# One joint block inverse for two recurrences, its diagonal blocks picked by DMA, and small work moved to GpSimd

## The chip, the cores and the metric

The kernel runs on one core of a Trainium2 chip. The metric is the device time of one execution in microseconds. Its engines are TensorE (PE; PEld is its weight load), VectorE (DVE), ScalarE (ACT), GpSimd (POOL) and SyncE (SP), which here issues all DMAs. Each runs its own queue of instructions in order, and waits at an instruction whose operands are not there.

## The reference

One step of a decoder layer for 1024 prompt tokens and 8 x 4 sample tokens. A projection `z = rmsnorm(x) @ w_in` feeds three mixers, whose outputs are gated, merged and followed by a feed-forward part. The change is in two of the mixers:

```
branch A (gated DeltaNet, 4 heads of 128 x 128, chunks of tokens)
  L    = strict_lower((k*beta) k^T * decay)      A = I + L
  u, w = A^-1 [v*beta | k*beta*exp(gc)]          attn = q k^T * decay
  per chunk:  vnew = u - w S;   o = (q exp(gc)) S + attn vnew
              S = S*exp(gc_last) + (k exp(gc_last - gc))^T vnew
branch B (RWKV-7, 8 heads of 64 x 64), per token
  S = S diag(w) - (S kk)(kk*a)^T + v k^T;   o = S r
  then group norm of o, bonus, gate
```

Branch B is solved by chunks of 64 tokens too, so each branch needs the inverse of unit triangular systems: 128 x 128 for each head and 128 tokens of A, 64 x 64 for each head and 64 tokens of B.

## The kernel before

Tokens lie along the free dimension, channels along partitions. `k.gemm` streams a weight in 128-column chunks through `wraw`; ScalarE and GpSimd split it in a high and a low half (`whi`, and `wlo` at L303), and TensorE takes three matmuls of 352 columns for each piece (L312 to L314, into PSUM tile `g`). These are the large products. Their chunks for the input projection and, later, for the merge gates are fed between the recurrences.

The recurrences run over two halves of the heads, and in each over nine segments: eight of 128 prompt tokens and one with the 32 sample tokens. `gdn_seg` is branch A's unit, two heads at once; `rwkv_seg` is branch B's, four blocks of two heads. That makes 18 pairs of units. Each unit has three parts, split by `yield`: the preparation with the block inverse `inv16`; the solve on top of it and the step of the state; and the output norm. The driver emits a unit's first part, then what is left of the unit before it, first for B and then for A. A scheduler then orders each engine's instructions from this order, so that instructions of different units and of the large products interleave.

`inv16` inverts the 16 x 16 diagonal blocks of all systems of a unit. VectorE masks the matrix to its diagonal blocks (L779), sums them to 16 columns (L782) and adds the unit diagonal (L783). A DMA writes the result to DRAM (L786) and another reads it back with each block's 256 numbers in all 16 partitions of the block (L788). Then 15 steps of a product (L795, tile `i16t`) and a sum (L796, tile `i16u`) give the inverse, row by row. `tri32` combines 16-blocks to 32-blocks by TensorE, and the code behind it goes on to 64 for B and to 128 for A. `inv16`, `tri32` and the tiles exist once with the suffix `r` (branch B) and once with `g` (branch A).

`rsqrt` is a Newton root, one instruction and three rounds of three (L592 to L594). It is used three times in a pair: for the keys' norms of A (tiles `nwyg`, `nwtg`), for A's output norm (`nwyo`, `nwto`) and for B's group norm (`nwyr`, `nwtr`). `BK` holds branch B's scaled keys. `LA` holds for each head of A the matrix L and the matrix attn side by side, `kv` its keys and values with tokens on partitions.

Of the kernel before, what the change touches and what calls it, by code (L numbers as in the profile page):

```python
# [95 lines left out]
def _consts():  # L96
# [33 lines left out]
    add("amk", np.where(p[:, None] > p[None], 0, NEG))  # L130
# [3 lines left out]
    add("amks", np.where(same4 & (t32[:, None] > t32[None]), 0, NEG))  # L134
# [238 lines left out]
def build(tc, ap):  # L373
    nc = tc.nc
    with ExitStack() as ctx:
# [209 lines left out]
        def rsqrt(x, shape, tag):  # L585

            yi = k.tile(mp, shape, "nwy" + tag, 2, I32)
            t = k.tile(mp, shape, "nwt" + tag, 1)
            V.tensor_scalar(out=yi, in0=x.bitcast(I32), scalar1=-0.5, scalar2=1597463007.0, op0=ALU.mult, op1=ALU.add)
            y = yi.bitcast(F32)  # L590
            for _ in range(3):
                V.tensor_tensor(out=t, in0=y, in1=y, op=ALU.mult)  # L592
                V.scalar_tensor_tensor(out=t, in0=t, scalar=-0.5, in1=x, op0=ALU.mult, op1=ALU.mult)
                V.scalar_tensor_tensor(out=y, in0=t, scalar=1.5, in1=y, op0=ALU.add, op1=ALU.mult)  # L594
            return y
# [63 lines left out]
        sc = c2.tile([128, 7, 9, 4], F32, name="sc")  # L659
        tg = c2.tile([128, 9, 4], F32, name="tg")  # L660
        for r, bs in ((128, slice(0, 8)), (32, slice(8, 9))):
            gc_, lb_ = gcb[:r, bs, :, 0], gcb[:r, bs, :, 1]
            A.activation(out=sc[:r, 0, bs], in_=gc_, func=AF.Exp, bias=k.c("lnh", r))
            A.activation(out=sc[:r, 1, bs], in_=lb_, func=AF.Exp, bias=k.c("lnh", r))
            V.scalar_tensor_tensor(out=sc[:r, 2, bs], in0=sc[:r, 0, bs], scalar=-2.0, in1=sc[:r, 1, bs], op0=ALU.mult, op1=ALU.mult)
            V.tensor_tensor(out=tg[:r, bs], in0=gla[:r, bs], in1=gc_, op=ALU.subtract)
            A.activation(out=sc[:r, 3, bs], in_=tg[:r, bs], func=AF.Exp, bias=k.c("lnh", r))
            V.tensor_copy(sc[:r, 4, bs], gc_)
            V.tensor_scalar(out=sc[:r, 5, bs], in0=gc_, scalar1=-1.0, scalar2=-2.0 * LN2, op0=ALU.mult, op1=ALU.add)
            V.tensor_scalar(out=sc[:r, 6, bs], in0=sc[:r, 1, bs], scalar1=0.5, scalar2=None, op0=ALU.mult)  # L670
# [98 lines left out]
        def inv16(fam, src, mask, nb, r, rows):  # L769


            srcs = src if isinstance(src, list) else [src]
            nq = srcs[0].shape[2]
            m = (k1() if fam == "r" else k.tile(mp, [128, SEG], "vv", 1))[:r, :nb * nq * 16]
            m = m.rearrange("p (b q c) -> p b q c", b=nb, q=nq)
            w = r // len(srcs)
            for i, a in enumerate(srcs):
                x = slice(w * i, w * i + w)
                V.tensor_tensor(out=m[x], in0=a, in1=mask[x].unsqueeze(1).unsqueeze(3).to_broadcast([w, nb, nq, 16]), op=ALU.mult)  # L779
            e16 = k.c("e16", r).unsqueeze(1).to_broadcast([r, nb, 16])  # L780
            c16 = k.tile(mp, [128, 4, 16], "i16c" + fam, 1)[:r, :nb]
            V.tensor_reduce(out=c16, in_=m.rearrange("p b q c -> p b c q"), axis=AXX, op=ALU.add)  # L782
            V.tensor_tensor(out=c16, in0=c16, in1=e16, op=ALU.add)  # L783
            k.n += 1
            dr = tc.dram_tile([r, nb * 16], F32, name=f"scr_i{k.n}")
            S.dma_start(dr, c16.rearrange("p b c -> p (b c)"))  # L786
            mb = k.tile(mp, [128, 1024 if fam == "r" else 512], "i16b" + fam, 1)[:r, :256 * nb]
# [18 lines left out]
        def tri32(fam, nb, l_of, transposed, u16):  # L806
# [735 lines left out]
```

## Time and profile before

| | us |
|---|---|
| median of 3 runs (lowest, highest) | 2314.09 (2312.11, 2326.05) |
| the profiled execution | 2314.56 |
| its span | 2312.8 |
| TensorE, VectorE, ScalarE, GpSimd busy in the span | 2203.3, 1310.6, 833.8, 303.7 |
| mean granted TensorE clock | 0.955 |

The span is the stretch from the first to the last instruction of the profiled execution. Busy time of an engine is the union of its instructions' durations. The two levels of TensorE's clock are 2.4 and 1.2 GHz, and a granted clock of 0.9 is a mean over both.

### The profile page before, as it was taken

How to read it: one execution, taken by the hardware profiler on the slowest of the kernel's cores; microseconds unless marked ns; L12 is line 12 of the kernel's file. 1: busy time of each engine (PE TensorE's matmuls, PEld its weight loads, DVE VectorE, ACT ScalarE, POOL GpSimd, SP SyncE). 2: the span in 40 equal slices, each digit the busy share in tenths (PEclk: the TensorE clock that was granted, in tenths of full speed). 3: DMA queues.
4: the chain of work that ended last, by engine and by line, in shares of the span. 5: the costliest groups of instructions: out<-in, count | busy, mean ns of one | idle time of the engine just before them, and what ended most of it. 6: DMA issues, size and time to landing. Idle time of an engine off the chain costs nothing. (4 is left out here: it accounts for less than half of the span.)

```text
span 2312.8 us, 43191 instructions
## 1 busy us (share of the span) xinstructions
PE 2203.3 (95%) x16747; PEld 2040.8 (88%) x16747; DVE 1310.6 (57%) x4204; ACT 833.8 (36%) x1969; POOL 303.7 (13%) x439
## 2 busy tenths in 40 slices
PE   8998998999998989899999999999999999999997
PEld 7998997777777767777799999989999999999997
DVE  7454247779888877787930167374333333343446
ACT  5466344344444434443432222253222122122234
POOL 3113222111121020111112100130000000000003
PEclk9999999789989988898999999999999999999999
DMA  4213224222323233223242354331111111111114
GB/s 144 67 60 101 100 99 119 87 87 79 98 79 99 81 107 91 84 73 85 77 142 93 124 196 140 122 113 44 46 48 47 46 47 46 46 46 46 46 49 150
DMA packets 138328, 199.82 MB, mean 86 GB/s; under 512 B 23880, under 2 KB 76488, under 8 KB 138124
## 3 DMA queue, kind: packets, MB, share of 16 engines
q1 hardware_dynamic: 138124, 197.07, 27.3%
q8 instruction: 132, 2.16, 0.4%
q14 instruction: 72, 0.59, 0.1%
HBM read 152.32 MB, written 44.70 MB: 85 GB/s over the span
## 5 line engine op out<-in xcount | busy, mean ns | idle before, releaser
L312 PE MATMUL g<-hhi,whi 128*128 128x352 f32 x2568 | 859.0, 335 | 11.2 <-DVE z L366 10.5
L314 PE MATMUL g<-hhi,wlo 128*128 128x352 f32 x2568 | 855.1, 333 | 0.9 <-POOL wlo L303 0.9
L313 PE MATMUL g<-hlo,whi 128*128 128x352 f32 x2472 | 822.6, 333 | 4.3 <-DVE hlo L505 2.6
L312 PEld LDWEIGHTS g<-hhi,whi 128*128 128x128 f32 x2568 | 493.0, 192 | 24.2 <-DVE z L366 12.5
L314 PEld LDWEIGHTS g<-hhi,wlo 128*128 128x128 f32 x2568 | 492.2, 192 | 10.8 <-issue 2.2
L313 PEld LDWEIGHTS g<-hlo,whi 128*128 128x128 f32 x2472 | 474.4, 192 | 15.0 <-DVE hlo L505 4.6
L302 ACT CAST whi<-wraw 128x512 fp32r<-128x512 f32 x326 | 201.3, 619 | 508.4 <-PE g L313 496.7
L303 DVE TENSOR_TENSOR wlo<-wraw,whi 128x512 fp32r<-128x512 f32 x216 | 151.6, 702 | 199.0 <-ACT whi L302 194.2
L312 PE MATMUL g<-ahi,whi 128*128 128x352 f32 x768 | 248.5, 324 | 0.0
L314 PE MATMUL g<-ahi,wlo 128*128 128x352 f32 x768 | 248.4, 323 | 0.0
L313 PE MATMUL g<-alo,whi 128*128 128x352 f32 x768 | 247.8, 323 | 0.0
L303 POOL TENSOR_TENSOR wlo<-wraw,whi 128x512 fp32r<-128x512 f32 x110 | 148.8, 1354 | 547.4 <-ACT whi L302 468.2
L1504 DVE TENSOR_TENSOR x<-g,x 128x352 f32<-128x352 f32 x192 | 100.3, 524 | 200.4 <-PE g L314 200.2
L1443 POOL TENSOR_TENSOR acc<-acc,sq 128x352 f32<-128x352 f32 x36 | 37.0, 1027 | 910.1 <-ACT sq L1442 743.8
L312 PEld LDWEIGHTS g<-ahi,whi 128*128 128x128 f32 x768 | 144.3, 188 | 0.2
L314 PEld LDWEIGHTS g<-ahi,wlo 128*128 128x128 f32 x768 | 144.3, 188 | 0.1
L313 PEld LDWEIGHTS g<-alo,whi 128*128 128x128 f32 x768 | 144.3, 188 | 0.1
L1493 DVE TENSOR_TENSOR rl<-rl,g 128x352 f32<-128x352 f32 x96 | 49.8, 518 | 130.9 <-ACT rl L1492 130.9
L1492 ACT ACTIVATE rl<-g 128x352 f32<-128x352 f32 x96 | 44.4, 463 | 136.3 <-PE g L314 136.3
L795 DVE TENSOR_TENSOR i16tr<-i16ur,i16br 128x8 f32<-128x8 f32 (+5 forms) x270 | 64.2, 238 | 38.0 <-DMA i16br<-scr_i 37.3
L1495 DVE TENSOR_TENSOR alo<-rl,ahi 128x352 fp32r<-128x352 f32 x96 | 50.3, 524 | 47.5 <-ACT ahi L1494 47.5
L1494 ACT CAST ahi<-rl 128x352 fp32r<-128x352 f32 x96 | 46.7, 487 | 63.2 <-DVE rl L1493 63.2
(383 smaller groups left out, 3048.8 us busy)
## 6 DMA issues: line engine op xcount, KB each, us to landing
wraw<-win SPq DMA_DIRECT2D x126, 256.0 KB
wraw<-wdn SPq DMA_DIRECT2D x80, 256.0 KB
wraw<-wup SPq DMA_DIRECT2D x64, 256.0 KB
scr_t<-z SPq DMA_DIRECT2D x24, 528.0 KB
tgl<-scr_t SPq DMA_DIRECT2D x24, 528.0 KB
scr_za<-z SPq DMA_DIRECT2D x16, 528.0 KB
i16br<-scr_i SPq DMA_DIRECT2D x16, 512.0 KB
wraw<-wout SPq DMA_DIRECT2D x32, 256.0 KB
```

The source lines that it names most:

```text
L302: self.A.copy(hi, r3)
L303: self.lo_eng.tensor_tensor(out=lo, in0=r3, in1=hi.bitcast(F32), op=ALU.subtract)
L312: T.matmul(ps, whi(k), xhi(k), start=start and k == ks[0], stop=False)
L313: T.matmul(ps, whi(k), xlo(k), start=False, stop=False)
L314: T.matmul(ps, wlo(k), xhi(k), start=False, stop=stop and k == ks[-1])
L795: V.tensor_tensor(out=t[:, :, 0:c + 1], in0=u[:, :, 0:c + 1], in1=w, op=ALU.mult)
L1443: (V if last else P).tensor_tensor(out=acc[g], in0=acc[g], in1=sq, op=ALU.add)
L1492: A.activation(out=rl, in_=ps, func=AF.Relu)
L1493: V.tensor_tensor(out=rl, in0=rl, in1=ps, op=ALU.mult)
L1494: A.copy(a[:, gl(g)], rl)
L1495: V.tensor_tensor(out=b[:, gl(g)], in0=rl, in1=a[:, gl(g)].bitcast(F32), op=ALU.subtract)
L1504: V.tensor_tensor(out=x2[c][:, gl(g)], in0=ps, in1=x2[c][:, gl(g)], op=ALU.add)
```

## The change

Branch A's system is now kept in transposed form, as B's has always been, so that one routine can treat the blocks of both. `gdn_seg` writes `LA` with one instruction for each head (matrix and attn share one exponential, whose sign is folded into the scalars), and leaves the key norm's scaling of `kv` to GpSimd. `inv16` and `tri` are called once for a pair. `inv16` no longer masks and sums: 16 DMAs copy the 16 x 16 diagonal blocks from `GM` and `LA` to DRAM, eight of each, and one DMA reads them back. The 15 steps run on six blocks at once, four of B and two of A (four in all in the two sample segments of B). `tri` does the two levels of the solve for all six, and the last level for A's 128 x 128 alone; its copies out of PSUM are shared between VectorE and ScalarE. The roots of A's output norm and of B's group norm, one of the two halves of `BK`, and the expansion of `X64` go to GpSimd, where each round of a root is four instructions. The driver emits B's preparation, then solve and state step of the older pair's B, then A's preparation, the joint inverse, and the older pair's A.

```diff
-        def rsqrt(x, shape, tag):
+        def rsqrt(x, shape, tag, E):
...
             for _ in range(3):
-                V.tensor_tensor(out=t, in0=y, in1=y, op=ALU.mult)
...
+                E.tensor_tensor(out=t, in0=y, in1=y, op=ALU.mult)
+                if E is V:
...
+                else:
+                    E.tensor_tensor(out=t, in0=t, in1=x, op=ALU.mult)
+                    E.tensor_scalar(out=t, in0=t, scalar1=-0.5, scalar2=1.5, op0=ALU.mult, op1=ALU.add)
+                    E.tensor_tensor(out=y, in0=t, in1=y, op=ALU.mult)
...
+        def inv16(J):
+            GM, LA, nb, nt = J["GM"], J["LA"], J["nb"], J["nb"] + 2
             k.n += 1
+            dr = tc.dram_tile([128, nt, 16], F32, name=f"scr_i{k.n}")
+            for g in range(8):
+                x = slice(16 * g, 16 * g + 16)
+                q = 16 * (g % 4)
+                S.dma_start(dr[x, 0:nb], GM[x, g // 4, 0:nb, q:q + 16])
+                S.dma_start(dr[x, nb:nt], LA[x, :, 0, 16 * g:16 * g + 16])
+            mb = k.tile(mp, [128, 1536], "i16b", 1)[:, :256 * nt]
+            S.dma_start(mb, dr.rearrange("(g k) b c -> g (k b c)", k=16).unsqueeze(1).to_broadcast([8, 16, 256 * nt]))
...
             for c in range(1, 16):
...
+                V.tensor_tensor(out=t[:, :, 0:c], in0=u[:, :, 0:c], in1=mb[:, 0:c, :, c].rearrange("p k b -> p b k"), op=ALU.mult)
                 V.tensor_reduce(out=u[:, :, c], in_=t[:, :, 0:c + 1], axis=AXX, op=ALU.add)
+            J["u16"] = u
...
+        def tri(J):
...
+            XT, X, y, z = tl("ixt"), tl("ix"), tl("iy"), tl("iz")
+            expand(XT, u16, k.c("h2"), nt, 2)
             V.transpose(out=w(X), in_=w(XT))
+            ps = rps32()
+            for b in range(nt):
                 for i in range(4):
+                    T.matmul(ps[Q[i], b], part(i, b, 0), X[Q[i], b], start=True, stop=True)
+            V.tensor_tensor(out=y, in0=ps, in1=k.c("lo16").unsqueeze(1).to_broadcast([128, nt, 32]), op=ALU.mult)
+            ps = rps32()
+            for b in range(nt):
                 for i in range(4):
+                    T.matmul(ps[Q[i], b], y[Q[i], b], XT[Q[i], b], start=True, stop=True)
+            V.tensor_tensor(out=XT, in0=ps, in1=XT, op=ALU.add)
             V.transpose(out=w(X), in_=w(XT))
+            W = J["W"] = k.tile(mp, [128, 6, 64], "inv", 2)[:, :nt]
+            expand(W, XT, k.c("d2"), nt, 2)
...
-                for src, j in ((kk, 0), (zk, 1)):
+                for src, j, e in ((kk, 0, P), (zk, 1, V)):
...
-                rs = rsqrt(mv[:, 1], [128, nb], "r")
+                rs = rsqrt(mv[:, 1], [128, nb], "r", P)
...
-                V.tensor_tensor(out=kv[:n, 1, 0:nb], in0=kv[:n, 1, 0:nb], in1=rk.unsqueeze(2).to_broadcast([n, nb, 128]), op=ALU.mult)
+                P.tensor_tensor(out=kv[:n], in0=kv[:n], in1=sl[:, 1:3].unsqueeze(3).to_broadcast([n, 2, 2, 128]), op=ALU.mult)
...
+                    V.scalar_tensor_tensor(out=LA[:n, b, :, :n], in0=pgv, scalar=sl[:, 0, b:b + 1],
+                                           in1=ar[:n, :n].unsqueeze(1).to_broadcast([n, 2, n]), op0=ALU.mult, op1=ALU.mult)
...
-                rs = rsqrt(oss[:n, :nb], [n, nb], "o")
+                rs = rsqrt(oss[:n, :nb], [n, nb], "o", P)
...
+            next(ur)
+            if old:
+                tri(old[0])
+                chain(old[1])
+            next(ug)
+            inv16(J)
+            if old:
+                chain(old[2])
+            old = J, ur, ug
```

The order of each engine's instructions can be read from the two built programs. Counted over all of it, VectorE has 4206 instructions before and 2906 now, GpSimd 444 and 984, SP 806 and 1040 DMAs, TensorE 13782 matmuls and 13878. Between the first matmul of a pair and the last one stand 1878 matmuls of the large products before, and 2091 now. Three places follow.

VectorE before, in the middle of the second half: B's steps (`i16tr`) stand one by one between instructions of both branches, among them A's mask and sum.

```order
L779 TENSOR_TENSOR vv_11402<-LA_11347,con 128x256
L795 TENSOR_TENSOR i16tr_11117<-i16ur_11115,i16br_11113 128x4x2
L1051 COPY UV_11148<-sr_11242 64x2x64
L796 TENSOR_REDUCE i16ur_11115<-i16tr_11117 128x4
L782 TENSOR_REDUCE i16cg_11404<-vv_11402 128x32
L795 TENSOR_TENSOR i16tr_11117<-i16ur_11115,i16br_11113 128x4x3
L819 TENSOR_TENSOR iyg_11458<-rg_11449,con 128x64
```

VectorE now, at the end of an inverse and in the solve behind it (`ixt`, `ix`, `iy`, `iz` and `inv` are its tiles, `rr` its PSUM). Line numbers are those of the changed kernel.

```order
L792 TENSOR_TENSOR i16t_9968<-i16u_9967,i16b_9965 128x6x15
L793 TENSOR_REDUCE i16u_9967<-i16t_9968 128x6
L799 TENSOR_TENSOR ixt_10121<-i16u_9967,con 128x192
L820 STREAM_TRANSPOSE ix_10122<-ixt_10121 128x192
L825 TENSOR_TENSOR iy_10123<-rr_10127,con 128x192
L830 TENSOR_TENSOR ixt_10121<-rr_10153,ixt_10121 128x192
L831 STREAM_TRANSPOSE ix_10122<-ixt_10121 128x192
L799 TENSOR_TENSOR inv_10180<-ixt_10121,con 128x384
L838 COPY iz_10124<-rr_10182 32x192
L851 COPY inv_10180<-rr_10197 32x6x32
L799 TENSOR_TENSOR TT_10218<-inv_10180,con 128x256
```

The steps now follow each other, 30 in a row but for the first few, and the solve follows them; between two of its instructions stand only matmuls.

SP before, around one inverse of A: one write of the blocks (L786), one read of them (L788).

```order
L786 DMA scr_i_11407<-i16cg_11404 128x32
L1379 DMA scr_t<-z_14388 128x1056
L297 DMA wraw_14665<-win 128x512
L788 DMA i16bg_11409<-scr_i_11407 128x1x512
L867 DMA ll_12080<-scr_l 128x2x32
L1160 DMA vl_12865<-scr_za_93 128x2x128
L865 DMA zv_11553<-scr_zb_91 128x2x128
L1109 DMA scr_y<-k_1862_11330 128x128 x2
L297 DMA wraw_14671<-win 128x512
L1322 DMA scr_y<-zg_10819 128x128 x2
```

SP now, around one joint inverse: seven of the eight picks from `GM` (the eighth is ahead), then the eight from `LA`, then the read (L784).

```order
L781 DMA scr_i_10412<-GM_10101 16x4x16 x7
L1359 DMA scr_t<-z_13572 128x1056
L291 DMA wraw_13763<-win 128x512
L291 DMA wraw_13849<-win 128x512
L900 DMA zr_10518<-scr_zb_91 128x2x128
L1174 DMA vl_11306<-scr_za_93 128x2x128
L782 DMA scr_i_10412<-LA_10364 16x2x16 x8
L1167 DMA gr_11302<-scr_g 128x128 x2
L291 DMA wraw_13855<-win 128x512
L784 DMA i16b_10429<-scr_i_10412 128x1x1536
```

One write became sixteen, and the read of both branches waits for all of them.

GpSimd before, in the second half, over about one pair (`wlo` is the low half of a weight chunk, `k`, `og` the gated output of B):

```order
L791 COPY i16ur_12683<-con 128x64
L791 COPY i16ug_12935<-con 128x32
L303 TENSOR_TENSOR wlo_14760<-wraw_14757,whi_14759 128x512
L906 COPY wc_12625<-k_2120_12618 128x4
L303 TENSOR_TENSOR wlo_14766<-wraw_14763,whi_14765 128x512
L303 TENSOR_TENSOR wlo_14852<-wraw_14849,whi_14851 128x512
L1107 TENSOR_TENSOR k_2064_12375<-k_2064_12375,og_11606 128x256
```

GpSimd now, at the same place, up to the first round of a root (`nwyo`, `nwto`):

```order
L297 TENSOR_TENSOR wlo_13760<-wraw_13757,whi_13759 128x512
L790 COPY i16t_10906<-con 128x96
L789 COPY i16u_10905<-con 128x6
L799 TENSOR_TENSOR x_1585_10198<-ix_10122,con 64x128
L1197 TENSOR_TENSOR kv_10365<-kv_10365,gsl_10394 128x512
L297 TENSOR_TENSOR wlo_13766<-wraw_13763,whi_13765 128x512
L941 COPY wc_10547<-k_1649_10540 128x4
L583 TENSOR_SCALAR nwyo_10495<-oss_10466 128x2
L586 TENSOR_TENSOR nwto_10496<-nwyo_10495 128x2
L591 TENSOR_TENSOR nwto_10496<-nwto_10496,oss_10466 128x2
L592 TENSOR_SCALAR nwto_10496<-nwto_10496 128x2
L593 TENSOR_TENSOR nwyo_10495<-nwto_10496,nwyo_10495 128x2
```

The root goes on for two more rounds, and the group norm's root stands right behind it; `kv` stands ahead of both.

## Rows read from the trace of the kernel before

**Rows 1.** The page, 40 equal slices of the span: VectorE's busy share, in tenths.

```profile
DVE  7454247779888877787930167374333333343446
```

**Rows 2.** Windows: us, busy (count) PE PEld DVE ACT POOL, clock, DMA, GB/s.

```profile
345.00:1180.00 835.00, 766.13 (x7956) 624.73 (x7955) 673.43 (x3106) 355.55 (x1105) 143.09 (x221) 0.89 0.31 88
1200.00:1300.00 100.00, 99.91 (x623) 99.62 (x623) 2.80 (x2) 23.28 (x45) 23.51 (x18) 1.00 0.32 108
```

**Rows 3.** The same, tile g alone: PE PEld DVE ACT.

```profile
345.00:1180.00 835.00, 427.98 (x1912) 325.20 (x1911) 2.20 (x12) 35.78 (x80) 0.89 0.31 88
1200.00:1300.00 100.00, 99.91 (x623) 99.62 (x623) 0.00 (x0) 11.77 (x26) 1.00 0.32 108
```

**Rows 4.** Window 345 to 1180: VectorE on i16tr, then on i16tg.

```profile
345.00:1180.00 835.00, 112.48 (x540) 0.89 0.31 88
...
345.00:1180.00 835.00, 95.92 (x540) 0.89 0.31 88
```

**Rows 5.** Groups by line and form, 345 to 1180: diagonal blocks picked.

```profile
L779 DVE TENSOR_TENSOR k<-GM,con 64x256 f32<-64x256 f32 x32 | 14.2, 443 | 0.5
...
L782 DVE TENSOR_REDUCE i16cr<-k 128x64 f32<-128x256 f32 x16 | 9.3, 578 | 0.0
...
L779 DVE TENSOR_TENSOR vv<-LA,con 128x256 f32<-128x256 f32 x16 | 7.2, 449 | 0.0
```

**Rows 6.** The same view: steps of the roots.

```profile
L592 DVE TENSOR_TENSOR nwtr<-nwyr 128x4 f32<-128x4 f32 x48 | 10.3, 214 | 0.2
...
L594 DVE SCALAR_TENSOR_TENSOR nwyr<-nwtr,nwyr 128x4 f32<-128x4 f32 x48 | 8.0, 166 | 0.1
```

**Rows 7.** The same view: BK and LA.

```profile
L927 DVE TENSOR_TENSOR BK<-k,k 64x256 f32<-64x256 f32 x32 | 14.6, 455 | 0.5
...
L1194 DVE SCALAR_TENSOR_TENSOR LA<-rg,gsl,ar 128x128 f32<-128x128 f32 x32 | 11.0, 344 | 0.4
...
L1196 DVE TENSOR_TENSOR LA<-rg,ar 128x128 f32<-128x128 f32 x32 | 8.9, 279 | 0.1
```

**Rows 8.** The same view: the solve on top of the 16-blocks.

```profile
L803 DVE TENSOR_TENSOR invr<-ixtr,con 128x256 f32<-128x256 f32 x16 | 6.2, 386 | 0.0
...
L803 DVE TENSOR_TENSOR ixtr<-i16ur,con 128x128 f32<-128x128 f32 x16 | 5.5, 343 | 0.0
...
L985 DVE COPY izr<-rr 32x128 f32<-32x128 f32 x16 | 4.5, 283 | 7.1 <-PE rr L984 6.7
...
L992 DVE COPY invr<-rr 32x128 f32<-32x128 f32 x16 | 4.5, 279 | 5.6 <-PE rr L991 5.5
```

**Rows 9.** The same view, GpSimd: two sizes.

```profile
L1107 POOL TENSOR_TENSOR k<-k,og 128x256 f32<-128x256 f32 x16 | 14.4, 898 | 61.8 <-DVE k L1106 27.7 <-DVE i16ug L796 19.0 <-DVE i16tg L795 15.1
...
L906 POOL COPY wc<-k 128x4 f32<-128x4 f32 x16 | 5.0, 309 | 122.2 <-ACT k L901 108.7 <-DVE i16tr L795 11.0 <-DVE N L1080 2.6
```

**Rows 10.** Timeline: start, us, engine, instruction; GpSimd and VectorE, first and last meeting.

```profile
351.38 1.92 POOL L1282 TENSOR_TENSOR S<-S,glb 128x1024 f32<-128x1024 f32 x1 [0.85 <-PE sg L1255]
...
351.47 2.94 DVE L1138 SCALAR_TENSOR_TENSOR z<-z,z 128x1056 f32<-128x1056 f32 x1
...
1174.25 1.27 POOL L303 TENSOR_TENSOR wlo<-wraw,whi 128x512 fp32r<-128x512 f32 x1 [1.05 <-ACT whi L302]
...
1174.42 1.11 DVE L594 SCALAR_TENSOR_TENSOR nwyr<-nwtr,nwyr 128x4 f32<-128x4 f32 x1
```

**Rows 11.** Lines 786, 788 and tile i16br: ns min/median/max, first and last start, waits.

```profile
L786 SPq DMA_DIRECT2D scr_i<-i16cr x18: 319/538/1917, 365.9 to 1124.6; - x18
L786 SPq DMA_DIRECT2D scr_i<-i16cg x18: 314/320/384, 368.8 to 1136.8; - x18
...
L795 DVE TENSOR_TENSOR i16tr<-i16ur,i16br x270: 135/206/1342, 375.4 to 1145.2; 128x8 f32<-128x8 f32 x9, 128x16 f32<-128x16 f32 x9, 128x24 f32<-128x24 f32 x9, 128x32 f32<-128x32 f32 x9
L788 SPq DMA_DIRECT2D i16br<-scr_i x18: 620/626/657, 367.3 to 1126.1; - x18
...
  DMA i16br<-scr_i: 37.3, 16
```

More of the change, by code (lines that the diff above doesn't have):

```diff
@@ new lines, in tri @@
+            V.transpose(out=w(X), in_=w(XT))
+            W = J["W"] = k.tile(mp, [128, 6, 64], "inv", 2)[:, :nt]
+            expand(W, XT, k.c("d2"), nt, 2)
+            ps = rps32()
+            for b in range(nt):
+                for a in (0, 2):
+                    T.matmul(ps[Q[a + 1], b], part(a, b, 1), X[Q[a], b], start=True, stop=True)
+            V.tensor_copy(z[Q[1]], ps[Q[1]])
+            A.copy(z[Q[3]], ps[Q[3]])
+            ps = rps32()
+            wide = not J["asamp"]
+            if wide:
+                X64 = k.tile(mp, [64, 2, 64], "x64", 1)
+                expand(X64, X[0:64, nb:], k.c("d2", 64), 2, 2, P)
+                ps64 = rps("g")[:, :64].rearrange("p (b c) -> p b c", b=2)
+                for b in range(2):
+                    T.matmul(ps64[Q[1], b], XT[Q[1], nb + b], z[Q[1], nb + b], start=True, stop=True)
@@ new lines, in tri @@
+            for b in range(nt):
+                for a in (0, 2):
+                    T.matmul(ps[Q[a], b], z[Q[a + 1], b], XT[Q[a + 1], b], start=True, stop=True)
+            V.tensor_copy(W[Q[0], :, 32:64], ps[Q[0]])
+            A.copy(W[Q[2], :, 32:64], ps[Q[2]])
+            if not wide:
+                J["TT"] = W[:, nb:]
+                return
+            A.copy(X64[Q[1], :, 0:32], ps64[Q[1]])
+            TT = J["TT"] = k.tile(mp, [128, 2, 128], "TT", 2)
+            expand(TT, W[:, nb:], k.c("q2"), 2, 2)
@@ new lines, in tri @@
+            ps = rps("g")[:, :128].rearrange("p (b c) -> p b c", b=2)
+            for b in range(2):
+                T.matmul(ps[H[1], b], LA[H[0], b, 0, 64:128], X64[:, b], start=True, stop=True)
+            y64 = k.tile(mp, [128, 2, 64], "y64", 1)
+            A.copy(y64[H[1]], ps[H[1]])
+            ps = rps("g")[:, :128].rearrange("p (b c) -> p b c", b=2)
+            for b in range(2):
+                T.matmul(ps[H[0], b], y64[H[1], b], W[H[1], nb + b], start=True, stop=True)
+            A.copy(TT[H[0], :, 64:128], ps[H[0]])
@@ L1328, in build, with chain @@
         SEGB.insert(6, (T0, TS))
[L1329 to L1337 removed]
+        def chain(u):
+            next(u)
+            next(u, None)
+        ra = rb = old = None
         for i in range(18):
```

218 lines of the change are left out of this document (57 added, 161 removed).

## The prediction

> **What bounds the kernel now.** I read the page's slices first, then the windows of the stage that the change edits, then groups, timeline and queue in it. TensorE is busy for 2203 of the 2313 us, but in slices 7 to 20 VectorE too is at seven to nine tenths [rows 1], and there the granted TensorE clock is 0.89 in the mean, so part of the time at the lower of its two levels [rows 2]. That is the stage of the 18 pairs of segments, from 345 to 1180 us. In it the matmuls of the large products (tile g) are 1912, against 623 in each 100 us of the stage behind it, where nothing else runs [rows 2, 3]. At 99.9 / 623 = 0.160 us each they would need 306 of the 835 us. All matmuls cover 766 us, those of g 428, so the small ones 338 [rows 2, 3]; 306 + 338 = 644, and near 190 us is TensorE waiting, or running at the lower level of its clock. VectorE is busy for 673 us of the 835, 37.4 of the 46.4 us that one pair takes (835 / 18), and idle for 9.0 [rows 2]. So the pair is paced by VectorE with its waits, and TensorE fills what it can with waiting products. I argue from the pair's period: what leaves VectorE shortens it, until TensorE's own need is the bound.
>
> **VectorE's part, step by step.** *Block inverse.* The two inverses run 540 instructions each, 112.5 and 95.9 us together 208 [rows 4]. The joint one runs 540 in all over six blocks at once. Interleaved they take 0.208 us each (112.48 / 540); each now stands right behind the one whose result it needs, and is up to half wider, so I take 0.25: 135 us, 73 less (the ends: 0.20 and 0.30, 27 us either way). *Picking the diagonal blocks*: L779 14.2 + 7.2, L782 9.3 for each branch (one of two like groups shown), and behind each an addition of 0.2 us, 7 in all; with the sample segments 50 us [rows 5]; all of it goes. *Two of three roots*: a root is three rounds of L592, L593, L594, 48 instructions a line, from 8.0 to 10.3 us (the ends shown) [rows 6]; 9.2 x 3 lines x 2 roots = 55, with their first line and the sample segments 66 us. *Half of BK*: one of two like groups, 14.6 us and the sample's 2, makes 16 [rows 7]. *LA*: two instructions of 0.344 and 0.279 us for 32 blocks, 19.9 us, become one of 256 elements, about 0.42, 13 us; one of two mask additions of L1196's size goes (9), the scaling of kv leaves (7), a small product comes (3): together 20 us [rows 7]. *The solve on top*: 20 VectorE instructions for two full blocks become nine; 11 x 0.283 (L985) x 16 = 50, less the nine being wider (at L803 128 more elements cost 386 - 343 = 43 ns, and some of the nine grow by more; 0.08 x 9 x 18 = 13) and the sample segments' new solve (6): 31 [rows 8]. The sum: 73 + 50 + 66 + 16 + 20 + 31 = 256 us; 673 becomes 417.
>
> **What GpSimd gives back.** It gets 13 small instructions for each root, two roots for each of 18 pairs: 468. The nearest row is its copy of 4 elements, 0.309 us with waits in it [rows 9]; I take 0.23, 108 us. Two BK products of 64x256 (L1107 has that size, 0.898; I take 0.7) make 25, kv of 512 elements, as the 1.27 of wlo, 23, the rest some 5: 160 us on top of 143. This is not free for VectorE. An instruction of VectorE with two operands in SBUF that starts while GpSimd works ends only after GpSimd has let go: L594 needs 0.16 us, and took 1.11, ending 0.01 us behind wlo [rows 10]. I added what instructions of VectorE that began inside one of GpSimd took over the lower quartile of their group: 61.6 us, in 90 instructions, the first and the last of which are shown, each under its GpSimd instruction; GpSimd's durations in the stage add to 148 us [rows 10]. That is 0.42 us for each us; 160 x 0.42 = 67 us. The ends: 0, where the two never meet, and 160, where every us shuts VectorE out. 417 + 67 = 484, or 26.9 us a pair. The Trainium skill, "GPSIMD Engine Reference", section 1 (Specifications), says that GpSimd shares its SBUF interfaces with VectorE and contends with VectorE instructions that have two SBUF inputs; this speaks against moving small products there. It names no size: by the page alone the sum could be anything from 417 to 577 us, by the rows it is 484, and the trace agrees that there is contention (1.11 us for 0.16).
>
> **Waits.** The 9.0 us of idle time a pair stay, and three are added. The order of VectorE has the 30 steps and the solve in one piece, with nothing of another branch between, so the solve's round trips over TensorE lie open. L985 and L992 each end one, and have 7.1 and 5.6 us of idle time before them, 0.4 a trip where other work covers the rest [rows 8]. Uncovered I put a trip at 0.85 us, for weights, matmuls and two hand-overs; four are 3.4 a pair, of which 1.1 are paid already (12.7 / 16 = 0.8, and some 0.3 at two other trips): plus 2.3, with ends of 0 and 4. GpSimd's two roots stand one behind the other ahead of the product that needs the group norm's root (L1111 of the changed kernel), 26 instructions of 0.23 or 6 us, and VectorE has some 4 us of other rows there: plus 2, with ends of 0 and 5. The transfer: behind LA stand eight picks on SP's queue at 0.32 us of issue, 2.6 us, then the read of 768 KB where 512 and 256 were read apart. Now the read is issued 1.4 us behind the write (365.9 and 367.3 us, the first pair), the first step follows 8.1 us later (375.4), and VectorE idles 37.3 us in 16 such waits, 2.1 a pair [rows 11]. The new path is 2.6 + 1.4 + 10 for the larger read, 14 us and what else SP has in line, and the order has some 31 rows of VectorE between LA and the first step, 13 us at 0.42 each (L1196 0.279 to L927 0.455). Plus 1.7 beside the 2.1 now paid, with ends of 0 and 6. The period is then 26.9 + 9.0 + 2.3 + 2 + 1.7 = 41.9 us; 18 make 754, 81 us less than 835.
>
> **TensorE's part.** The order places 2091 matmuls of the large products between the first small matmul of the pairs and their last one, where 1878 stood, and so 213 fewer behind it, at 0.160 us: 34 us less after the stage. In the stage they need room: 306 + 34 + 338, and 96 more small matmuls, some 5, are 683 us, 38 a pair. That is under 41.9, so VectorE and its waits still pace, at nine tenths of TensorE. The picks themselves, 288 issues of 0.32 us, are 92 us on SP over 754 [rows 11]; I put them at nothing beyond the 1.7, since SP's loads of weights and segments run ahead of their use by a buffer; if that cover were gone, a load behind a pair's picks would come 5 us late. ACT gets the solve's other copies and gives up scaled ones: it is busy for 356 of 835 us [rows 2], and I put it at nothing.
>
> The profiled execution took 2314.56 us, 1.8 more than its span of 2312.8, and the median of the runs is 2314.09, so no correction is due: 2314.6 - 81 - 34 = **2199.6, say 2200 us**.
>
> **Rivals.** *TensorE becomes the bound*: everything added to VectorE's waits is hidden, the period falls to TensorE's 38 us, the stage to 683: 2314.6 - 152 - 34 = 2129 us. For it: the small matmuls' 338 hold lower-clock time that a denser stage may not pay; against it: one queue that runs in order, and round trips in every pair. *The shared interface decides*: all 160 us of GpSimd come out of VectorE, 417 + 160 = 577, 32.1 + 15 = 47.1 us a pair, 848 in all: 2314.6 + 13 - 34 = 2294 us. For it: 13 instructions in a row leave no gap for VectorE; against: many instructions of VectorE (reductions, copies, those that read PSUM) need no second SBUF operand. The Trainium skill's page, "GPSIMD Engine Reference", section 1, is the rule behind this rival, and would not exclude it. *The pair's period stays*, because the chain through TensorE and not VectorE's work paces it: 835 stays, and 34 go: 2281 us. For it: VectorE is idle a fifth of the time now. Against: it idles in pieces of 1 to 3 us, at DMA and TensorE trips. *Slower*: the joint inverse makes one chain of what were two that covered each other: LA, eight or more picks, read, 30 steps, solve, both branches' states. If picks of GM stand behind LA too (16 x 0.32 = 5.1 us, 2.5 more), if SP holds the read back behind another wait (3 us) and the roots hold L1111 for 4 instead of 2, the period is 41.9 + 7.5 = 49.4, 889 us, and the time 2314.6 + 54 - 34 = 2335; it decides from (835 + 34) / 18 = 48.3 us a pair. Against it: both old chains already had a read each, and branch A's order puts 31 rows under it.
>
> **How the numbers follow.** The forecast, periods of 39 to 45 us (2150 to 2255 us), gets 0.56; TensorE as the bound 0.08; the stage as long as now 0.14; the shared interface 0.12; slower 0.10. A measurement here tells about 1% from no change (the runs shown differ by 0.6%). Faster by over 1%, under 2291: the first three, most of them, and a little of the fourth: 0.79; within 1%: 0.12; slower: 0.09. The range, 2135 to 2300 us, leaves out the slower rival and the last end of the fastest one; the unknown costs inside it are the 27 us of the steps, the 67 of the interface (0 to 160) and 0 to 6 us a pair of the transfer.
>
> **What would show it.** In the profile of the changed kernel the stage should last 750 us, VectorE be busy near 480 us in it, the roots' instructions on GpSimd average near 0.23 us, steps 0.25 us, and matmuls of g be near 2125 in the stage. If VectorE is near 480 and the stage is as long as before, the waits were undercounted: then the first step should idle for over 5 us behind the read, or L1111 behind GpSimd. If VectorE is near 570, the interface did it. If TensorE shows hardly a gap, its need was the bound. The prediction is wrong above all if the picks' landing is slower than the write of one tile was, which no row of this trace shows.

## The result and the profile after

The changed kernel takes 2378.35 us (median of 4 runs, 2373.57 to 2385.66), beside 2317.57 of the kernel before (4 runs): a ratio of 1.026, 95% interval 1.022 to 1.031. It is slower by 61 us, where 2200 was forecast and the range ended at 2300: the time moved the other way. The profiled execution is the slowest of the four, 2385.66 us; its span of 2383.9 is 71 longer than that of before.

VectorE over the span in 40 slices, the line that answers to [rows 1]:

```profile
DVE  7454347566666675665542037656343333433437
```

Its share fell from seven to nine tenths to five to seven, and the stage lasts some two slices longer. The windows of the changed kernel, the stage (345 to 1284 us, where the last small matmul of the recurrences lies) and 100 us behind it, with the columns of [rows 2]:

```profile
345.00:1284.00 939.00, 817.32 (x8325) 689.13 (x8323) 574.95 (x1806) 342.57 (x1066) 309.48 (x764) 0.86 0.30 82
1300.00:1400.00 100.00, 100.00 (x629) 99.75 (x628) 12.19 (x15) 25.66 (x47) 17.18 (x13) 1.00 0.39 123
```

The same stage, tile g alone, as [rows 3]:

```profile
345.00:1284.00 939.00, 449.55 (x2091) 370.65 (x2091) 2.18 (x12) 39.90 (x88) 0.86 0.30 82
```

The stage now holds 2091 large matmuls, the number that the order gave, and what lies behind it is shorter by 36 us (2383.9 - 1284 = 1100 beside 2312.8 - 1177 = 1136): that term was right, to 2 us. All of the error lies in the stage, which is 104 us longer than before (939 - 835) and holds 179 more of the large matmuls (2091 - 1912). It takes 939 us, or 52.2 a pair, where 754 and 41.9 were forecast. VectorE is busy for 575 us, 31.9 a pair (26.9 forecast), and idle for 364, 20.2 a pair (15.0 forecast). So both halves of the sum failed, by about 5 us a pair each. TensorE's granted clock is 0.86 in the mean, 0.89 before, and it stands idle for 122 us of the stage (939 - 817), 69 before.

What VectorE waits for in the stage (the waiting instruction, what it waits for, us in all, times, longest; the seven largest):

```profile
DVE k L1111 <- POOL nwyr L593: 55.1, 18, 6.5
DVE zg L1293 <- PE sg L1292: 36.8, 14, 4.1
DVE UV L1065 <- ACT UV L1064: 28.5, 28, 2.1
DVE inv L851 <- PE rr L850: 23.6, 15, 2.8
DVE iy L825 <- PE rr L824: 22.3, 17, 2.9
DVE i16t L792 <- DMA i16b<-scr_i: 21.7, 6, 6.7
DVE ixt L830 <- PE rr L829: 21.3, 16, 1.9
```

What TensorE and, in the last fence, ScalarE wait for there, in the same columns:

```profile
PE sg L1292 <- ACT oa L1291: 40.8, 16, 4.9
PE sr L1116 <- DVE k L1111: 25.9, 12, 5.3
PE rr L824 <- DVE ix L820: 23.2, 9, 5.6
PE rr L976 <- POOL BK L962: 9.8, 8, 2.4
```

```profile
ACT oa L1291 <- POOL nwyo L593: 52.6, 18, 5.1
```

The same places in the kernel before, where VectorE made both roots (its L1097, L1102, L1317, L1318 and L1319 are the changed kernel's L1111, L1116, L1291, L1292 and L1293):

```profile
PE sr L1102 <- DVE k L1097: 6.6, 6, 2.1
PE sg L1318 <- ACT oa L1317: 1.8, 4, 0.7
```

```profile
ACT oa L1317 <- DVE nwyo L594: 17.6, 9, 3.2
```

The longest wait of VectorE is L1111, for the group norm's root on GpSimd: 55.1 us, where the same product of before had no idle time ahead of it. The same wait passes on to TensorE at L1116 (25.9, 6.6 before). The second root, of A's output norm, is used by ScalarE (L1291), which stands for 52.6 us at it (17.6 before), TensorE behind that for 40.8 (L1292, 1.8 before), and VectorE behind TensorE for 36.8 (L1293, 7.3 before). The first step (L792) waits for its read only 21.7 us, less than the 37.3 of [rows 11]. The solve's five waits (L825, L830, L838, L851 and the one behind ScalarE's copy, 22.3 + 21.3 + 14.2 + 23.6 + 10.2) are 91.6 us, 5.1 a pair.

### The profile page after: what moved, and what is told of

Same layout as the page of the kernel before. It is cut to its first block, busy times and chain, and to the rows that moved or that the text cites. A ratio compares the mean times of both kernels' runs of the same rounds, so it can differ in the third digit from the quotient of the medians.

```text
span 2383.9 us, 43121 instructions
## 1 busy us (share of the span) xinstructions
PE 2225.8 (93%) x16939; PEld 2077.3 (87%) x16939; DVE 1214.3 (51%) x2904; ACT 814.5 (34%) x1917; POOL 467.2 (20%) x979
## 4 chain that ended last, share of the span: by engine, by line
PE 55%; DVE 5%; POOL 4%; issue 2%; DMA 2%; ACT 1%; SPq 0%; DVEq 0%; POOLq 0%; ACTq 0%
PE g L306 16%; PE g L307 16%; PE g L308 16%; DVE i16t L792 1%; DMA i16b<-scr_i 1%; PE sr L1041 1%; DVE i16u L793 1%; PE rr L976 1%; POOL wlo L297 0%; PE rg L1204 0%; POOL BK L962 0%; PE sr L1116 0%; DVE ahi L1502 0%; PE sg L1238 0%; PE rr L824 0%
## 5 line engine op out<-in xcount | busy, mean ns | idle before, releaser
L306 PEld LDWEIGHTS g<-hhi,whi 128*128 128x128 f32 x2568 | 499.6, 195 | 16.9 <-DVE z L360 8.3
L308 PEld LDWEIGHTS g<-hhi,wlo 128*128 128x128 f32 x2568 | 499.5, 195 | 10.1 <-issue 2.3
L307 PEld LDWEIGHTS g<-hlo,whi 128*128 128x128 f32 x2472 | 482.0, 195 | 11.3 <-DVE hlo L499 2.7
L792 DVE TENSOR_TENSOR i16t<-i16u,i16b 128x6 f32<-128x6 f32 (+5 forms) x270 | 84.2, 312 | 28.6 <-DMA i16b<-scr_i 21.7
L1356 ACT ACTIVATE z<-g 128x352 f32<-128x352 f32 x72 | 33.3, 463 | 111.5 <-PE g L308 111.0
```

What stands on the lines that cost most here:

```text
L306: T.matmul(ps, whi(k), xhi(k), start=start and k == ks[0], stop=False)
L307: T.matmul(ps, whi(k), xlo(k), start=False, stop=False)
L308: T.matmul(ps, wlo(k), xhi(k), start=False, stop=stop and k == ks[-1])
L792: V.tensor_tensor(out=t[:, :, 0:c], in0=u[:, :, 0:c], in1=mb[:, 0:c, :, c].rearrange("p k b -> p b k"), op=ALU.mult)
L1356: A.activation(out=tz[:, gl(g)], in_=ps, func=AF.Tanh, scale=0.5)
```

## The experiments

Three theories stood at the start. R: the wait for GpSimd's roots is the price. C: the joint inverse and solve are one serial chain, and that is the price. W: VectorE's amount of work sets the time, so that whatever comes back to it costs. Three more come in with later runs: D, the picks' transfer is the price; S, the serial inverse and solve are; and the overlap of VectorE's instructions. Ratios are to the kernel before, with their 95% intervals. The kernel before took 2317.57 us beside the changed kernel, 2310.33 beside runs 1 to 4, 2318.66 beside 5 to 8 and 2313.88 beside 9 to 12; a difference between two versions is therefore taken from their ratios.

| run | median us | ratio |
|---|---|---|
| changed kernel | 2378.35 | 1.026 (1.022 to 1.031) |
| 1 roots back on VectorE | 2355.35 | 1.018 (1.013 to 1.022) |
| 2 BK, kv, X64 back on VectorE | 2357.92 | 1.021 (1.016 to 1.026) |
| 3 both | 2339.07 | 1.012 (1.008 to 1.015) |
| 4 kernel before, roots on GpSimd | 2390.33 | 1.034 (1.030 to 1.038) |
| 5 as 3, mask for the picks | 2329.60 | 1.006 (1.002 to 1.010) |
| 6 as 3, picks from LA issued by ScalarE | 2338.71 | 1.011 (1.007 to 1.015) |
| 7 as 3, two inverses | 2333.95 | 1.008 (1.005 to 1.010) |
| 8 as 3, steps in two halves | 2327.22 | 1.004 (1.001 to 1.008) |
| 9 as 5, steps in two halves | 2322.63 | 1.005 (1.002 to 1.007) |
| 10 kernel before, roots a second time on GpSimd | 2338.54 | 1.012 (1.008 to 1.015) |
| 11 as 5, two inverses | 2327.28 | 1.007 (1.004 to 1.010) |
| 12 as 11, two solves | 2311.47 | 0.999 (0.996 to 1.002) |

**1. Roots back on VectorE.**

```diff
-                rs = rsqrt(mv[:, 1], [128, nb], "r", P)
+                rs = rsqrt(mv[:, 1], [128, nb], "r", V)
-                rs = rsqrt(oss[:n, :nb], [n, nb], "o", P)
+                rs = rsqrt(oss[:n, :nb], [n, nb], "o", V)
```

> The changed kernel with both moved roots back on VectorE (as two-step rounds of three instructions); all else as changed. Theory R (roots): TensorE waited 66.7 us at lines 1292 and 1116 for what hangs on GpSimd's roots, 8.4 us at the same two places before; about 58 us come back, so 2378 - 58 = 2320 us (2305 to 2335). Theory C (chain): the 30 dependent steps and the solve's open trips set the pair's period, and the roots' wait lies beside them: 2365 to 2385. Theory W (work): VectorE's own busy time paces, and it gets some 40 to 55 us back: 2410 to 2430.

1.018 beside 1.026: faster by 0.9%, some 20 us and not 58 (the two intervals just touch), and not slower. W falls. R has the sign, but part of the wait moves elsewhere: VectorE's idle time ahead of the first step rises from 21.7 to 47.4 us.

**2. BK, kv and X64 back on VectorE.**

```diff
-                for src, j, e in ((kk, 0, P), (zk, 1, V)):
+                for src, j, e in ((kk, 0, V), (zk, 1, V)):
-                P.tensor_tensor(out=kv[:n], in0=kv[:n], in1=sl[:, 1:3]...
+                V.tensor_tensor(out=kv[:n], in0=kv[:n], in1=sl[:, 1:3]...
-                expand(X64, X[0:64, nb:], k.c("d2", 64), 2, 2, P)
+                expand(X64, X[0:64, nb:], k.c("d2", 64), 2, 2, V)
```

> The changed kernel with GpSimd's half of BK, the scaling of kv and the expansion of X64 back on VectorE; the roots stay on GpSimd. R: TensorE's 9.8 us of wait at line 976 for GpSimd's BK come back, and the roots' wait stays: 2360 to 2375. C: no change, 2370 to 2385. W: VectorE gets 40 to 50 us of instructions back: 2400 to 2420.

1.021, 0.5% or some 12 us less; its interval overlaps that of the changed kernel, so alone it is not clear. TensorE's waits for the roots stay (46.4 at L1292, 25.0 at L1116).

**3. Both edits.**

> Both edits of the two runs before: nothing of what was moved stays on GpSimd, so what is left is the joint inverse with its picks by DMA and the new order of emission. R: 2305 to 2325, near the kernel before. C: 2360 to 2385, since the joint inverse alone is at fault. W: 2430 to 2470.

1.012, some 33 us less than the changed kernel and clear of it; still 1.2% behind the kernel before. What had been moved to GpSimd accounts for more than half of the loss, the roots (0.9%, run 1) for more of it than the other work (0.5%, run 2), though neither of these two is clear by itself; what remains is left for C. TensorE's two longest waits and VectorE's longest in this run:

```profile
PE rr L824 <- DVE ix L820: 28.9, 10, 7.2
PE sg L1292 <- ACT oa L1291: 16.4, 6, 4.5
```

```profile
DVE i16t L792 <- DMA i16b<-scr_i: 66.7, 18, 5.8
```

The roots' waits are gone or small. VectorE now stands behind the read in all 18 pairs, and TensorE at the solve's first matmul, behind the last step.

**4. The kernel before, roots on GpSimd.**

```diff
-                rs = rsqrt(mv[:, 1], [128, nb], "r")
+                rs = rsqrt(mv[:, 1], [128, nb], "r", P)
-                rs = rsqrt(oss[:n, :nb], [n, nb], "o")
+                rs = rsqrt(oss[:n, :nb], [n, nb], "o", P)
```

> The kernel before with the two roots (A's output norm, B's group norm) on GpSimd in the changed kernel's form, and nothing else of the change. R: the wait appears here too: 2314 + 58 = 2372 (2345 to 2385). C: it lies beside the two covered chains: 2305 to 2325. W: VectorE loses 40 to 60 us of work: 2260 to 2280.

2390 us: this one part, in which the prediction saw 66 us of relief for VectorE, makes the kernel before slower by 3.4%, no less than the whole change does (2.6%; the intervals just touch). TensorE's waits show the same two places (its L1323 is the changed kernel's L1292, its L1107 is L1116):

```profile
PE sg L1323 <- ACT oa L1322: 39.0, 16, 4.4
PE sr L1107 <- DVE k L1102: 32.0, 14, 3.6
```

**10. The roots a second time, for nobody.** (The numbers are those of the table.)

```diff
+            if tag in "ro":
...
+                P.tensor_scalar(out=zi, in0=x.bitcast(I32), scalar1=-0.5, scalar2=1597463007.0, op0=ALU.mult, op1=ALU.add)
...
+                for _ in range(3):
+                    P.tensor_tensor(out=t, in0=z, in1=z, op=ALU.mult)
...
```

> The kernel before, with the two roots computed a second time on GpSimd in the changed kernel's 13 instructions; that result is used by nobody, and VectorE's own is used as before. GpSimd gets the same 468 small instructions as in the run with the roots moved (2390 us, ratio 1.034), but nobody waits for them. Theory R (the wait for GpSimd's result is the price): 0.998 to 1.006, 2310 to 2330. Shared interface (GpSimd's small instructions hold VectorE up, as the prediction priced with 0.42 us for each): 110 us of GpSimd give 40 to 45 us, 2355, 1.017 to 1.02; at the full 110 us 2420.

1.012: between the two theories in time, so of run 4's 3.4% about a third comes without anyone waiting for the root. But it is not VectorE that is held up. Summed as for [rows 10], instructions of VectorE that began inside one of GpSimd took 52.8 us over the lower quartile of their groups, in 79 instructions, where 61.6 in 90 stood before, although GpSimd's durations rose from 148 to 266 us. What rises is the wait for GpSimd's other work behind the roots in its queue, the product of L1117 (L1107 of before), from 15.1 us at the same copy before; ScalarE, then TensorE behind it (1.1 us there before):

```profile
ACT og L945 <- POOL k L1117: 38.4, 13, 5.1
```

```profile
PE rr L951 <- ACT og L945: 10.7, 6, 4.0
```

That the queue's delay is all of the 1.2% is read from this trace, not tried by itself.

**5. Mask, sum and one write for the 16 picks.**

```diff
-            for g in range(8):
...
-                S.dma_start(dr[x, 0:nb], GM[x, g // 4, 0:nb, q:q + 16])
-                S.dma_start(dr[x, nb:nt], LA[x, :, 0, 16 * g:16 * g + 16])
+            for h in range(2):
+                V.tensor_tensor(out=m[H[h]], in0=GM..., in1=k.c("d4")..., op=ALU.mult)
+            V.tensor_reduce(out=c16[:, 0:nb], ...)
...
+            V.tensor_tensor(out=m, in0=LA..., in1=k.c("d8")..., op=ALU.mult)
+            V.tensor_reduce(out=c16[:, nb:nt], ...)
+            S.dma_start(dr, c16)
```

> Built on the run with all moved work back on VectorE (2339 us). The 16 picks are replaced by mask, sum and one write as in the kernel before; the inverse stays joint. In that run the first step starts 17 us behind LA and VectorE idles 66.7 us in 18 waits for the read. Theory D (the picks' transfer is what is left of the loss): the way from LA to the first step falls to 12 us, the idle time there to about 40, and the time to 2310 to 2325, although VectorE gets some 45 us of instructions back. Theory S (the serial inverse and solve are what is left): the transfer is worth little and the 45 us of instructions cost: 2340 to 2375.

1.006: the interval touches that of run 3, so a gain is not clear, but the five more instructions of VectorE a pair cost nothing. The wait for the read is 68.0 us in 18 pairs, as long as with the picks (66.7), where D expected about 40: the time came out between the two theories, and D's reason is not there.

**6. Picks from LA issued by ScalarE.**

```diff
-                S.dma_start(dr[x, nb:nt], LA[x, :, 0, 16 * g:16 * g + 16])
+                A.dma_start(dr[x, nb:nt], LA[x, :, 0, 16 * g:16 * g + 16])
```

> Built on the 2339 us run: the eight picks from LA are issued by ScalarE's queue, not SP's, so that SP's queue holds eight issues fewer and the read waits only for them to land. D: the 4.5 us from LA's first pick to the end of the last, and the 2.6 us to the read, shrink; 2315 to 2330. S: 2333 to 2345. If ScalarE's own queue is delayed by eight issues of 0.3 us a pair (43 us): 2350 to 2370.

1.011, no difference from run 3, and VectorE still waits 64.0 us for the read (66.7 there): that the eight picks from `LA` are issued by SP is not what it waits for.

**7. Two inverses, joint solve.**

```diff
+            b0, nt = (0, J["nb"]) if fam == "r" else (J["nb"], 2)
             next(ur)
+            inv16(J, "r")
...
-            inv16(J)
+            inv16(J, "g")
```

> Built on the 2339 us run: the 16-blocks are inverted apart again, four of B behind its own eight picks and read, two of A behind theirs, 30 steps each; the solve stays joint. S: steps of the two interleave with other work again; their durations sum to 208 us, but overlapped they take VectorE no longer than the 120 us of the joint ones, so 2310 to 2330. D: each branch still waits for eight picks, but B's read is early: 2325 to 2340. By the sum of durations as in the prediction, 540 more instructions cost 60 to 75 us: 2400.

1.008: 540 more instructions on VectorE, and no slower than run 3, so the sum of durations, by which 2400 us were expected, is the wrong account; whether it is faster the intervals leave open.

**8. Steps in two halves.**

```diff
-                V.tensor_tensor(out=t[:, :, 0:c], ...)
-                V.tensor_reduce(out=u[:, :, c], ...)
+                for z in (slice(0, nt // 2), slice(nt // 2, nt)):
+                    V.tensor_tensor(out=t[:, z, 0:c], ...)
+                for z in (slice(0, nt // 2), slice(nt // 2, nt)):
+                    V.tensor_reduce(out=u[:, z, c], ...)
```

> Built on the 2339 us run: one read of six blocks as there, but each step is written as two products and two sums of three blocks each, which don't depend on each other. By the sum of durations 540 more instructions of 0.2 us are 100 us less the narrower ones' gain: 2390 or more. By overlap (an instruction starts before the one ahead of it has ended, unless it needs its result) VectorE is busy for no more than 20 us longer, and the time stays within 2330 to 2350.

1.004, clear of run 3 (1.0075 is the end of its interval, 1.0081 the start of run 3's) and faster by 0.75%, some 17 us. Why twice as many instructions cost so little can be read in the timelines (start, duration). Of the kernel before, one step of B (L795, L796) between other work:

```profile
644.29 0.17 DVE L796 TENSOR_REDUCE i16ur<-i16tr 128x2 f32<-128x24 f32 x1
644.37 0.23 DVE L829 STREAM_TRANSPOSE ixg<-ixtg 128x64 f32<-128x64 f32 x1
644.53 0.17 DVE L795 TENSOR_TENSOR i16tr<-i16ur,i16br 128x26 f32<-128x26 f32 x1
644.62 0.42 DVE L803 TENSOR_TENSOR TT<-ixtg,con 128x256 f32<-128x256 f32 x1
```

L796 starts at 644.29 and lasts 0.17, to 644.46, but the next instruction starts at 644.37. Of the changed kernel, two steps:

```profile
644.15 0.21 DVE L792 TENSOR_TENSOR i16t<-i16u,i16b 128x30 f32<-128x30 f32 x1
644.40 0.19 DVE L793 TENSOR_REDUCE i16u<-i16t 128x6 f32<-128x36 f32 x1
644.63 0.22 DVE L792 TENSOR_TENSOR i16t<-i16u,i16b 128x36 f32<-128x36 f32 x1
644.88 0.20 DVE L793 TENSOR_REDUCE i16u<-i16t 128x6 f32<-128x42 f32 x1
```

Each needs the result ahead of it and starts 0.03 us after that one has ended. So a narrow instruction takes about 0.08 us of VectorE there, and a step's instruction 0.24 here. The two groups of run 8 (busy is the union, so that mean times count is more), and then VectorE's busy time on the tile in that run, in run 3, on which it was built, and in the changed kernel:

```profile
L793 DVE TENSOR_TENSOR i16t<-i16u,i16b 128x12 f32<-128x12 f32 (+13 forms) x540 | 100.6, 221 | 59.6 <-DMA i16b<-scr_i 59.3
L795 DVE TENSOR_REDUCE i16u<-i16t 128x3 f32<-128x15 f32 (+13 forms) x540 | 77.7, 177 | 0.1
```

```profile
345.00:1256.00 911.00, 147.51 (x1080) 6.44 (x16) 0.90 0.32 87
```

```profile
345.00:1263.00 918.00, 131.47 (x540) 6.49 (x16) 0.91 0.32 87
```

```profile
345.00:1284.00 939.00, 140.05 (x540) 7.06 (x16) 0.86 0.30 82
```

In run 8 durations sum to 540 x (0.221 + 0.177) = 215 us and occupy 147.5; in run 3 131 occupy 131, and in the changed kernel 140 occupy 140. The Trainium skill, "Perfetto Trace Analysis", section "Optimizing Scalar/DVE Operations", gives a fixed data-access cost for each instruction and says that the profiled latency is about twice this, since the half in which the write is acknowledged overlaps with the next instruction. The rows agree where the next instruction doesn't need the result (0.08 of 0.17 us), and show that the overlap is gone where it does.

This explains why the steps of run 8 take VectorE only 16 us more than those of run 3, not why the kernel is faster. From the first product of an inverse to its last sum run 8's trace has 13.4 us in the mean, run 3's 14.5: 1.1 us a pair, 20 in all. But the two executions that were traced differ by only 5 us (2325.14 and 2330.57), and no run tries the chain's length by itself, so why run 8 is faster stays open.

**9. Mask and halves.**

> Mask, sum and one write for the 16 picks, and each step as two independent halves, both on top of the kernel with all moved work back on VectorE. That kernel stood at 1.012 of the kernel before, the mask alone at 1.006, the halves alone at 1.004. If the two are separate losses, the ratio is near 0.998 (2305 to 2320 us). If both only filled the same idle time of VectorE behind the read: 1.003 to 1.006 (2325 to 2335).

1.005, the same as with the halves alone. The gains of runs 5 and 8 don't add up, as they wouldn't if both filled the same idle time; what the picks cost by themselves lies between nothing (8 to 9) and 0.6% (3 to 5), and stays open.

**11 and 12. Mask and two inverses; then two solves.** Run 11 joins the edits of runs 5 and 7; what run 12 adds to it in the driver:

```diff
             if old:
-                tri(old[0])
+                tri(old[0], "r")
                 chain(old[1])
...
             if old:
+                tri(old[0], "g")
                 chain(old[2])
```

> Mask, sum and one write, and the two inverses apart again, each with its own read; the solve stays joint; all small work on VectorE. The joint form of this stood at 1.006. If B's early read and the interleaved steps cover each other: 0.996 to 1.002 (2305 to 2322). If the joint solve behind both is what orders the pair: 1.004 to 1.008.

> As the run with mask and two inverses, and the solve apart for B and A too, so that nothing is joint any more; what is left of the change is A's transposed form with one exponential and one instruction for LA. VectorE gets nine more instructions a pair. If the joint solve's open trips cost (85 us of VectorE's idle time in the changed kernel, 17 to 20 us before): 0.985 to 0.996 (2280 to 2305). If they lie in idle time anyway: no different from the run with mask and two inverses.

1.007, and then 0.999: taking the solve apart brings the kernel back to the time of before, with A's transposed form kept. VectorE's waits in the joint solve of run 11, then in the two of run 12:

```profile
DVE inv L859 <- PE rr L858: 14.8, 11, 2.3
...
DVE iy L833 <- PE rr L832: 10.4, 13, 1.2
```

```profile
DVE izr L846 <- PE rr L845: 5.4, 13, 1.9
...
DVE izg L846 <- PE rg L845: 5.2, 9, 1.2
...
DVE invr L859 <- PE rr L858: 4.6, 9, 1.5
```

The five waits of the joint solve are 45 us in run 11, the nine of the two solves 30.5 in run 12. VectorE's idle time in the stage falls from 209 to 150 us (916 - 707 and 819 - 669), so the solve's waits are a quarter of that. VectorE's busy time falls too, by 38 us, although it has 143 more instructions there: more of them overlap. The window of run 12, with the columns of [rows 2]:

```profile
345.00:1164.00 819.00, 761.28 (x8111) 622.63 (x8111) 669.46 (x3010) 348.72 (x1086) 146.28 (x251) 0.91 0.31 89
```

The edit also moves A's solve behind A's preparation, and the new order places 430 fewer large matmuls in the stage (1877 beside 2307), so the two stages' lengths can't be compared, only the kernels' times. Whether the two solves or the order that comes with them gave the 0.7% was not separated. No version that was run is clearly faster than the kernel before.

## Why the prediction was wrong

**What bounds the kernel now** was half right. VectorE with its waits paces the stage, but the two can't be split as the argument did: work that leaves VectorE shortens a pair only if nothing comes to wait for it. Run 4 gives it less to do and is slower; runs 7 and 8 give it 540 more instructions, and the time stays or falls.

**VectorE's part is the step that failed first.** The 256 us were sums of durations, and were taken from 673 us, which is a union. All durations of VectorE in the stage sum to 872 us before and 640 now, 232 less, near the 256; but its busy time falls only by 98, from 673 to 575, since 199 us of overlap became 65: in the stage before, 2483 of 3105 instructions start 0.06 to 0.10 us before the one ahead has ended, now 770 of 1806. The joint steps measured 0.26 us each (140 / 540), as forecast (0.25); the two inverses that they replace had durations of 208 us [rows 4] but added only 133 us to VectorE's busy time, when each instruction is counted from where the one ahead ends. By the same count the joint ones add 130. The joint inverse saved VectorE 3 us, not 73. With 98 us instead of 256 saved, and none of the 67 of contention below, VectorE is busy for 91 us more than forecast, 5.0 a pair.

**What GpSimd gives back**: the roots' instructions were well sized (0.20 to 0.25 us, two lines here, mean ns behind the busy time), the 67 us of contention not:

```profile
L586 POOL TENSOR_TENSOR nwtr<-nwyr 128x4 f32<-128x4 f32 (+1 forms) x54 | 13.4, 247 | 3.2
...
L592 POOL TENSOR_SCALAR nwto<-nwto 128x2 f32<-128x2 f32 (+1 forms) x54 | 11.5, 213 | 4.2
```

Counted as in [rows 10], VectorE lost 58.6 us in 94 instructions in the stage, 61.6 before, beside 319 us of GpSimd instead of 148. The price was carried over from long GpSimd instructions to small ones; here nothing was added. What GpSimd's small work cost was its queue and the wait for its results. Run 10 is the plainer case, since it adds nothing but the roots' small instructions (122 us): 52.8 us lost in 79. The rule of the Trainium skill ("GPSIMD Engine Reference", section 1) that the two share an interface agrees with [rows 10]; no growth of it is seen in the changed kernel.

**The waits are the step that failed second.** The prediction named L1111 behind the roots, at 2 us a pair, and did not ask who waits for the other root. L1111 idles 3.1 us a pair (55.1 / 18), near the forecast, but ScalarE at L1291, TensorE at L1292 and VectorE at L1293 (36.8 us) follow the root of A's norm. The timeline of GpSimd, ScalarE and TensorE at one such place shows it:

```profile
683.04 0.20 POOL L586 TENSOR_TENSOR nwto<-nwyo 128x2 f32<-128x2 f32 x1
683.32 0.19 POOL L583 TENSOR_SCALAR nwyr<-mv 128x4 int32<-128x4 int32 x1
683.59 0.20 POOL L591 TENSOR_TENSOR nwto<-nwto,oss 128x2 f32<-128x2 f32 x1
683.74 0.20 POOL L586 TENSOR_TENSOR nwtr<-nwyr 128x4 f32<-128x4 f32 x1
683.90 0.19 POOL L592 TENSOR_SCALAR nwto<-nwto 128x2 f32<-128x2 f32 x1
684.05 0.20 POOL L591 TENSOR_TENSOR nwtr<-nwtr,mv 128x4 f32<-128x4 f32 x1
684.21 0.20 POOL L593 TENSOR_TENSOR nwyo<-nwto,nwyo 128x2 f32<-128x2 f32 x1
...
684.44 0.69 ACT L1291 ACTIVATE oa<-oa,nwyo 128x128 f32<-128x128 f32 x2 [3.88 <-POOL nwyo L593]
...
684.89 0.14 PEld L1292 LDWEIGHTS sg<-con,oa 128*128 128x128 f32 x1 [4.13 <-ACT oa L1291]
```

The two roots also alternate in GpSimd's queue here, not one behind the other, so that the first is done later; ScalarE had stood 3.88 us at it and TensorE 3.84. Run 4 sizes the step: moving the roots was put at -66 us for VectorE, +45 of contention (108 x 0.42) and +36 for the wait (2 x 18), together +15, and measures +79 (0.034 x 2314). The solve's trips were put at 3.4 us a pair, and are 5.1 (4.5 for the four that were counted). The 0.85 us a trip came from no row; the four measure 1.1 in the mean (81.4 / 72). A trip with nothing in between is about as short as was put; what lengthens it are large products that stand ahead of it in TensorE's queue, and these the prediction left out. At L825 VectorE waits 0.6 to 1.1 us in the eleven pairs with no large matmul in between, and 2.0 to 2.9 in the four with 7 to 14. The one with 14, between the first two of these lines:

```profile
1149.98 0.31 DVE L820 STREAM_TRANSPOSE ix<-ixt 128x128 f32<-128x128 f32 x1
...
1152.70 0.33 PE L824 MATMUL rr<-ix,GM 32*32 32x32 f32 x16
...
1153.24 0.29 DVE L825 TENSOR_TENSOR iy<-rr,con 128x128 f32<-128x128 f32 x1 [2.95 <-PE rr L824]
```

No run changed that order by itself. The transfer was put at 3.8 with the part already paid, and is 1.2 (21.7 / 18); the picks' landing, of which the last sentence warned, wasn't it. The rest of the idle time, 5.8 of the 9.0 us a pair (less 2.1 for the read and 1.1 for trips), didn't stay but became 10.9 (20.2 - 5.1 - 3.1 - 1.2): nearly all of the 5.2 us by which the waits were short. In it VectorE waits at L1293 behind A's root (2.0 us a pair, 0.4 before), for ScalarE at L1065 (28.5 us in all, 8.4 at the same line before) and at other trips; that the removed work used to cover these is argued, not shown.

**TensorE's part** was right in its 34 us (36), and its bound was never reached: TensorE stands idle for 122 us of the stage.

**The rivals.** The slower one had the right sign, with 0.10, and in part the right mechanism: one chain in place of two that covered each other, and the roots at L1111. Its point of decision, 48.3 us a pair, was passed at 52.2. Of its three conditions only the roots' wait shows, at 3.1 us; the two on the picks and the read cost nothing that shows, since the first step waits less for its read than before. It was given too little because its base, 41.9, was too low by both failed steps. The rival by which the pair's period stays had this right, that VectorE's work alone doesn't pace the pair (runs 5, 7 and 8 add to it at no cost), but not that waits were added. The shared interface as the price is refuted by run 10.

**Where the 2.6% went**, by the runs in a row: work on GpSimd 1.4 (changed kernel to run 3), inverse and picks 0.5 (run 3 to 11), joint solve, with the order that goes with it, 0.7 (run 11 to 12). The first and the last are clear of their intervals, the middle one is not.

## What to carry to other kernels

Don't subtract durations from busy time: look in the timeline at how soon the next instruction starts, and count a removed instruction by that. Fusing two chains that run interleaved on one engine saves little when the fused one waits for each of its own results. Before a small chain moves to a slower engine, list who reads its last result on every engine and what stands in their queues: here two chains of 13 instructions held up three other engines.

## What was not expected of the hardware

Twice as many instructions on VectorE took little more time, and the kernel was faster by 0.75%: 1080 narrower instructions of the steps occupy 147.5 us in run 8, 540 wide ones 131.5 in run 3, since an instruction that doesn't need the result ahead of it starts about 0.08 us before that one has ended. And 171 us more of work on GpSimd in the stage (319 beside 148), 103 of it the roots' small instructions, held VectorE up no longer than before.
